# A decoder block's MLP: the down projection by Strassen's seven products in three of four quarters of the width

## Chip, cores and metric

One Trainium2 chip, one core of it. The metric is the device time of one execution in microseconds (us); lower is better. Engines: PE (matrix multiply), ACT (ScalarE), DVE (VectorE), POOL (GpSimd) and SP (which issues most DMA transfers). PE accumulates in PSUM banks of 128 x 512 float32; everything else lies in SBUF.

## The reference, cut to what matters

```python
D_MODEL, SEQ, D_FF = 1024, 512, 4096           # one batch, one layer, all float32
...
x = x + merged @ w_out[i]
h2 = rms_norm(x, norm_mlp_g[i])
x = x + jnp.square(jax.nn.relu(h2 @ w_mlp_up[i])) @ w_mlp_down[i]
return rms_norm(x, norm_final_g)
```

Two mixers (a gated MLP and a state-space scan) come first; the change leaves them alone. It is about the third line: 512 tokens, 1024 -> 4096 -> 1024.

## The kernel before

**Arithmetic.** A float32 product is made of three matmuls. Each operand is split into a rounded part and the rest (`whi`, `wlo` for weights, `ah`, `al` for activations): ACT casts the first (line 118), DVE subtracts (line 119), and `trio` / `mm3` issue lo x hi, hi x lo, hi x hi into one PSUM bank. A weight slab is a tile of 128 x 1024 (512 KB), so each slab costs one cast and one subtraction. `whi` and `wlo` have four buffers each.

**The MLP in quarters.** The hidden width is worked off in four quarters `qd` of 1024 channels. A list `items` says in which order PE takes the work, one slab per item:
- `("c", half)`: the up projection of the first 512 channels, eight plain blocks, in the first quarter only.
- `("p", u, k)`: the up projection of the `u`-th 512 channels is done by Strassen's method: the activation (channels x tokens) and the weights are cut into 2 x 2 blocks, and seven products `k` of block sums take the place of eight. An item is one product: 24 matmuls of 256 columns. The sums of activation blocks (`hq[1..7]`) are made once; the sums of weight blocks are made on the way in, by DMA: `Up.pump` has SP load raw blocks into eight tiles (`ut0` to `ut7`) as these come free, and `Up.sum` has POOL issue transfers that add into a tile (`accum_op`), four for each `u`, two of them from HBM and two from tile to tile. Three products are kept in SBUF (`keep`) and subtracted from a later bank by DVE; `act` then squares the relu on ACT and splits it into `ah`, `al`, which hold a whole quarter.
- `("d", qd, i)`: the down projection, plain: 24 matmuls of 512 columns per slab, eight slabs per quarter; the four finished banks of each half of the output are added to the tokens `x1` by DVE (`res_evac`). Two tiles `wraw` take the raw slabs.

**What sets the order.** The whole MLP stands in a hand-written order. At item `j` the loop first takes the results of item `j-1` out of PSUM, then issues POOL's additions that `sums_at[j]` lists, then splits the slab of item `j+3` (`slabs.take(3)`), then runs what `after[j]` holds (mostly `act`), and last issues the matmuls of `j`. Every engine works its own list strictly in that order. The last slabs go through `tok_major`, whose `fin(1)` also normalises and stores the output, the last token tile in two halves.

```python
items += [("d", qd, 0), ("p", 2 * qd + 1, 4)] + [("d", qd, i) for i in range(1, 8)]
...
for n, d in ((1, 8), (3, 7), (2, 5), (4, 3)) if u % 2 else ((1, 8), (3, 7), (2, 4), (4, 3)):
    sums_at[j - d].append((u, n))
```

Of the kernel before, what the change touches and what calls it, by code (L numbers as in the profile page):

```python
# [11 lines left out]
F32 = mybir.dt.float32  # L12
# [22 lines left out]
H2D = 0, 1.5, 2.5, 5.5, .4, 2.2, .6, 6, 8.5, 8.5  # L35
NR = 4

HALVES, B12 = (0, 2, 1, 3), 6
# [13 lines left out]
def block_kernel(ctx: ExitStack, tc: tile.TileContext, x, w_v, w_all, w_up, wspt, pvec, hvec, g_mix, g_mlp, g_fin, v_g, v_b,  # L52
# [21 lines left out]
    class Slabs:  # L74

        def __init__(self):
            self.ready, self.raws, self.loaded = [], [], 0
            self.todo = collections.deque()
            self.early = False

# [10 lines left out]
        def slab(self):  # L91
            if not self.raws:
                self.load()
            r = parts_of(self.raws.pop(0))
            while self.early and len(self.raws) < 2 and self.loaded < NV + w_all.shape[0]:
                self.load()
            return r
# [732 lines left out]
    class Up:  # L830

        def __init__(self):
            self.free, self.n, self.at = list(tiles), 0, {}

            self.todo = [(0, i) for i in HALVES] + [(1, i) for i in (0, 1, 2, 3, None)]
            self.todo += [(u, i) for u in range(2, 2 * NQ) for i in (2, 3, None, 0, 1)]

        def pump(self):
            while self.free and self.todo:
                t = self.free.pop(0)  # L840
                u, i = self.todo.pop(0)
                nc.sync.dma_start(t, w_up[4 * u + (2 if i is None else i)])
                self.at[u, i] = t

        def sum(self, u, n):

            def add(o, i):
                nc.gpsimd.dma_start(o, i, accum_op=ALU.add)

            self.pump()  # L850
            at = lambda i: self.at[u, i]
            if n == 1:
                add(at(None), w_up[4 * u + 3])
            elif n == 2:
                add(at(0), at(None))
            elif n == 3:
                add(at(2), w_up[4 * u])
            else:
                add(at(1), at(0))

        def make(self, u, k, pair=None):
            self.pump()
            i = {1: 0, 2: 1, 5: None, 6: 0, 3: 1, 7: 2, 4: 3}[k]
            r = parts_of(self.at[u, i], pair)
            if k > 2:
                self.drop(u, i)
            return r
# [11 lines left out]

    up = Up()  # L880
    later = [(0, 1), (0, 2), (0, 5), (0, 6), (0, 3), (0, 7), (1, 1), (0, 4), (1, 2), (1, 5), (1, 6), (1, 3), (1, 7)]


    items = []
    for qd in range(NQ):
        if qd == 0:
            items += [("c", 0)] + [("p", 1, k) for k in (1, 2)] + [("c", 1)] + [("p", 1, k) for k in (5, 6, 3, 7)]
        else:
            items += [("p", 2 * qd + u, k) for u, k in later]
        items += [("d", qd, 0), ("p", 2 * qd + 1, 4)] + [("d", qd, i) for i in range(1, 8)]  # L890
    place = {it: j for j, it in enumerate(items)}

    sums_at = collections.defaultdict(list)
    for u in range(2, 2 * NQ):
        j = place["p", u, 5]
        for n, d in ((1, 8), (3, 7), (2, 5), (4, 3)) if u % 2 else ((1, 8), (3, 7), (2, 4), (4, 3)):
            sums_at[j - d].append((u, n))
    for n, d in ((1, 0), (3, 0), (2, 0), (4, 1)):
        sums_at[d].append((1, n))
    slabs.todo.extend((lambda i=i: up.raw(i)) for i in HALVES)  # L900
    for it in items[4:]:
        slabs.todo.append(slabs.slab if it[0] == "d" else lambda it=it: up.make(*it[1:]))

# [18 lines left out]
    tiles.append(mp.tile([P, SL], F32, name="ut7"))  # L922
    up.free.append(tiles[7])
    gfb = mp.tile([P, DM], F32, name="gfb")
# [17 lines left out]
    def new_act(qd):  # L942
        aTs[qd] = tuple(ap.tile([P, KD, T], F32R, tag=n, name=n, bufs=1) for n in ("ah", "al"))

# [5 lines left out]
    def act(j, u, i, l, src):  # L950

        r_ = mp.tile([P, 2, 256], F32, tag="relu", name="relu", bufs=2)
        nc.scalar.activation(r_, src.rearrange("p (c t) -> p c t", c=2), AF.Relu)
        nc.scalar.activation(r_, r_, AF.Square)
        n = 4 * (u % 2) + 2 * i
# [18 lines left out]
    def act0(j, n, bank):  # L974

        r_ = mp.tile([P, T], F32, tag="relu", name="relu", bufs=2)
        nc.scalar.activation(r_, bank, AF.Relu)
        nc.scalar.activation(r_, r_, AF.Square)
        hi, lo = cut(aTs[0], n)
        nc.scalar.copy(hi, r_)  # L980
        last[j + 1].append(lambda: nc.vector.tensor_sub(lo, r_, hi.bitcast(F32)))

    sums = [[] for _ in range(NT)]

    def fin(nh):
        def evac(t, acc, part=None):
# [12 lines left out]
            if part == 0:  # L999
                return  # L1000
            rs = rms_scale(s)
            o = tiles[1 + t]
            a, b = slice(0, T), slice(T, DM)
            nc.scalar.activation(o[:, a], x1[:, t, a], AF.Copy, scale=rs)
            nc.vector.scalar_tensor_tensor(o[:, b], x1[:, t, b], rs, gfb[:, b], ALU.mult, ALU.mult)
            for c in (a, b):
                nc.sync.dma_start(out[t * P:(t + 1) * P, c], o[:, c])
        return evac
# [3 lines left out]
    for j, it in enumerate(items[:-4]):  # L1012

        if j and items[j - 1][0] == "p":
            _, u, k = items[j - 1]
            evac(j, u, k, BANK.get(k, lambda u: bank_a[u % 2])(u))
        if j == NR:
            wv.flush()
            nr_cm.__exit__(None, None, None)
            ap = ctx.enter_context(pool("act"))  # L1020
# [3 lines left out]
        for u, n in sums_at.pop(j, ()):  # L1024
            up.sum(u, n)
        for f in last.pop(j, ()):
# [3 lines left out]
        else:  # L1030
            w = slabs.take(3)
        for f in after.pop(j, ()):
            f()
# [18 lines left out]
        if it[0] == "p":  # L1052
            _, u, k = it
            if k == 1 and u % 2 == 0 and u:
                new_act(u // 2)
            bank = BANK.get(k, lambda u: bank_a[u % 2])(u)
            for c in range(2):
                for kt in range(4):
                    trio(bank[:, 256 * c:256 * c + 256], wk(w, 4 * c + kt), cut(hq[k], kt),
                         k in (1, 2, 5) and c == 0 and kt == 0, kt == 3)  # L1060
        else:
            _, qd, i = it
# [87 lines left out]
```

## Time and profile before

| | |
|---|---|
| median of 3 runs | 1063.15 us (1062.95 to 1064.41) |
| the profiled execution | 1063.19 us, of which its span (first to last instruction) is 1061.5 us |
| PE busy | 1048.0 us, 99% of the span |
| DVE, ACT, POOL busy | 640.8, 503.8, 163.5 us |
| DMA | 129.76 MB, mean 122 GB/s |

The durations further down are of the profiled execution, which stands 0.04 us from the median. The MLP begins near 725 us. A matmul's printed duration is longer than its distance from the next one, since matmuls overlap; distances are what count on PE.

### The profile page before, as it was taken

The numbers are of one execution on the slowest core, as the hardware profiler recorded it, in microseconds if no ns is written. First come the engines' busy times: TensorE is split into PE (matmuls) and PEld (weight loads), VectorE is DVE, ScalarE is ACT, GpSimd is POOL, SyncE is SP. The second block draws the span as 40 slices with busy tenths as digits, with TensorE's granted clock in tenths as the row PEclk, the third lists the DMA queues.
The fourth block names the chain that finished last, engine by engine and source line by source line (L and its number), as shares of the span: only waits on it lengthen the run. The fifth ranks groups of instructions, "written<-read, shape, count | busy, mean of one in ns | idle before, by whom it ended". The sixth has DMA issues, their size and how long they took to land.

```text
span 1061.5 us, 14620 instructions
## 1 busy us (share of the span) xinstructions
PE 1048.0 (99%) x5709; PEld 908.4 (86%) x5709; DVE 640.8 (60%) x1054; ACT 503.8 (47%) x750; POOL 163.5 (15%) x216
## 2 busy tenths in 40 slices
PE   8999999999999999999999999999999999999997
PEld 7988888888888888888888788879989989988986
DVE  5672455346897996647868975356635634634643
ACT  5743333234547556444465533245824724723742
POOL 3020000001432342300323410002001001101000
PEclk9999999999999999999999999999999999999999
DMA  6433225332333333233233233826737837835232
GB/s 210 141 119 119 80 80 139 99 100 80 100 99 108 106 91 111 82 120 99 80 109 97 71 122 94 299 63 175 206 116 178 219 100 169 232 116 119 62 99 80
DMA packets 39672, 129.76 MB, mean 122 GB/s; under 512 B 4529, under 2 KB 5297, under 8 KB 39602
## 3 DMA queue, kind: packets, MB, share of 16 engines
q1 hardware_dynamic: 35568, 114.13, 34.2%
q0 software_dynamic: 4032, 14.68, 7.5%
q8 instruction: 45, 0.74, 0.3%
q14 instruction: 25, 0.20, 0.1%
q10 hardware_dynamic: 2, 0.00, 0.0%
HBM read 119.30 MB, written 2.16 MB: 114 GB/s over the span
## 4 chain that ended last, share of the span: by engine, by line
PE 79%; DVE 11%; POOL 4%; issue 3%; ACT 2%; DMA 1%; POOLq 0%; SPq 0%; ACTq 0%; DVEq 0%
PE acc L147 15%; PE acc L149 15%; PE acc L148 15%; PE acc L155 14%; PE sm L149 5%; PE sm L147 5%; PE sm L148 5%; DVE cv L570 3%; DVE wlo L119 1%; DVE lm L610 1%; POOL xD L668 1%; PE sm L664 1%; POOL lm L613 1%; POOL yrs L677 1%; PE sm L155 1%
## 5 line engine op out<-in xcount | busy, mean ns | idle before, releaser
L119 DVE TENSOR_TENSOR wlo<-wraw,whi 128x1024 fp32r<-128x1024 f32 (+1 forms) x146 | 175.6, 1204 | 120.8 <-ACT whi L118 120.7
L118 ACT CAST whi<-wraw 128x1024 fp32r<-128x1024 f32 (+1 forms) x146 | 149.8, 1028 | 161.1 <-PE acc L149 73.4
L147 PE MATMUL acc<-hTl,whi 128*128 128x512 f32 x448 | 179.7, 401 | 0.0
L149 PE MATMUL acc<-hTh,whi 128*128 128x512 f32 x448 | 174.8, 390 | 0.0
L148 PE MATMUL acc<-hTh,wlo 128*128 128x512 f32 x448 | 174.6, 390 | 0.0
L119 DVE TENSOR_TENSOR wlo<-ut,whi 128x1024 fp32r<-128x1024 f32 x51 | 62.3, 1224 | 74.5 <-ACT whi L118 74.5
L149 PEld LDWEIGHTS acc<-hTh,whi 128*128 128x128 f32 x448 | 84.1, 188 | 18.0
L148 PEld LDWEIGHTS acc<-hTh,wlo 128*128 128x128 f32 x448 | 84.4, 188 | 15.0
L147 PEld LDWEIGHTS acc<-hTl,whi 128*128 128x128 f32 x448 | 84.4, 188 | 14.8
L147 PE MATMUL sm<-wlo,ah 128*128 128x512 f32 (+1 forms) x232 | 89.5, 386 | 0.0
L149 PE MATMUL sm<-whi,ah 128*128 128x512 f32 (+1 forms) x232 | 89.4, 386 | 0.0
L148 PE MATMUL sm<-whi,al 128*128 128x512 f32 (+1 forms) x232 | 89.4, 385 | 0.0
L118 ACT CAST whi<-ut 128x1024 fp32r<-128x1024 f32 x51 | 53.5, 1051 | 75.2 <-PE sm L149 52.6
L570 DVE SCALAR_TENSOR_TENSOR cv<-acc,pv,cv 128x511 f32<-128x511 f32 (+2 forms) x96 | 71.5, 745 | 29.3 <-ACT cv L568 28.5
L147 PE MATMUL acc<-wlo,hTh 128*128 128x512 f32 (+1 forms) x208 | 77.9, 375 | 0.2
L148 PE MATMUL acc<-whi,hTl 128*128 128x512 f32 (+1 forms) x208 | 75.6, 363 | 0.0
L149 PE MATMUL acc<-whi,hTh 128*128 128x512 f32 (+1 forms) x208 | 75.4, 364 | 0.0
L635 POOL TENSOR_TENSOR xdt<-xb,dt 128x256 f32<-128x256 f32 x32 | 21.9, 685 | 202.0 <-ACT xb L629 197.4
L149 PEld LDWEIGHTS sm<-whi,ah 128*128 128x128 f32 x232 | 43.6, 188 | 8.8
L148 PEld LDWEIGHTS sm<-whi,al 128*128 128x128 f32 x232 | 43.6, 188 | 8.5
L147 PEld LDWEIGHTS sm<-wlo,ah 128*128 128x128 f32 x232 | 43.6, 188 | 8.4
L147 PE MATMUL acc<-yBl,whi 128*128 128x512 f32 x128 | 50.6, 395 | 0.0
(310 smaller groups left out, 2330.7 us busy)
## 6 DMA issues: line engine op xcount, KB each, us to landing
wraw<-in_w_all SPq DMA_DIRECT2D x136, 512.0 KB, 3.6
ut<-in_w_up SPq DMA_DIRECT2D x39, 512.0 KB, 6.7
lm<-csd SPq DMA_DIRECT2D x32, 256.0 KB, 4.5
ut<-in_w_up POOLq DMA_DIRECT2D x14, 512.0 KB, 9.9
ut<-ut POOLq DMA_DIRECT2D x14, 512.0 KB, 4.7
wraw<-in_w_v SPq DMA_DIRECT2D x10, 352.0 KB, 3.2
x<-in_x SPq DMA_DIRECT2D x4, 512.0 KB, 7.2
out<-ut SPq DMA_DIRECT2D x8, 256.0 KB, 2.2
```

The source lines that it names most:

```text
L118: nc.scalar.copy(hi, raw)
L119: nc.vector.tensor_sub(lo, raw, hi.bitcast(F32))
L147: nc.tensor.matmul(o, st[0], mv[1], start=first, stop=False)
L148: nc.tensor.matmul(o, st[1], mv[0], start=False, stop=False)
L149: nc.tensor.matmul(o, st[0], mv[0], start=False, stop=last)
L155: nc.tensor.matmul(o, st[a], mv[b], start=first and i == 0, stop=last and i == 2, skip_group_check=True)
L570: nc.vector.scalar_tensor_tensor(cv[:, s_:], acc[:, :T - s_], cw[:, 3 - s_:4 - s_], cv[:, s_:], ALU.mult, ALU.add)
L610: nc.vector.tensor_scalar(lm[:, j, r, :], lm[:, j, r, :], ncs[:, 2 * hf + j, h0 + r:h0 + r + 1], None, ALU.add)
L613: nc.gpsimd.affine_select(lm, lm, pattern=[[0, 2], [0, R], [1, P]], base=0, channel_multiplier=-1, compare_op=ALU.is_ge, fill=-1e30)
L635: nc.gpsimd.tensor_tensor(xdt, xb4, bc(dt, c), ALU.mult)
L664: nc.tensor.matmul(yp[:, r * HD:(r + 1) * HD], lm[:, r, :], xdt[:, r, :], start=True, stop=True)
L668: nc.gpsimd.tensor_tensor(xD, xD, yv, ALU.add)
```

## The change

In quarters 0, 1 and 2 the down projection is done by seven products as well; quarter 3 keeps the eight plain slabs. An item `("s", qd, k, c)` is one half of the reduction of product `k`: 12 matmuls of 512 columns on one slab, so a product is two items. Its weights are block sums of `w_mlp_down`, made like those of the up projection: raw blocks loaded by SP, four adding transfers by POOL for each half `c`, eight for a quarter. Its activations are block sums too: a quarter's activation now stays whole in float32 (`a`); `down_sum` adds blocks of it in place on DVE, and `down_pair` splits a block into `prh` (ACT) and `prl` (DVE), three buffers of each. A product's two banks are added to or subtracted from `x1` at once by `down_evac`, and bank `a` runs on through products 1, 6, 7 and 4. For two of the `u` (3 and 5) the sums of weight blocks move from POOL's transfers to DVE (`ON_DVE`). The two `wraw` tiles join the eight `ut` tiles. Loads are ordered by when they are needed (`need`). At the very end one small DVE instruction per token tile is folded into another, and the last tile is stored in four pieces.

```diff
+ON_DVE, FINAL = (3, 5), (6, 7)
...
-            items += [("c", 0)] + [("p", 1, k) for k in (1, 2)] + [("c", 1)] + [("p", 1, k) for k in (5, 6, 3, 7)]
+            items += [("c", 0)] + [("p", 1, k) for k in (1, 2)] + [("c", 1)] + [("p", 1, k) for k in (5, 6, 7, 3, 4)]
...
-        items += [("d", qd, 0), ("p", 2 * qd + 1, 4)] + [("d", qd, i) for i in range(1, 8)]
+        if qd == NQ - 1:
+            items += [("d", qd, 0), ("p", 2 * qd + 1, 4)] + [("d", qd, i) for i in range(1, 8)]
+        else:
+            items += [("s", qd, 1, c) for c in range(2)] + [("p", 2 * qd + 1, 4)] * (qd > 0)
+            items += [("s", qd, k, c) for k in (5, 6, 2, 7, 3, 4) for c in range(2)]
...
+            ds = {1: at(5) - 8, 2: at(6) - 6, 3: at(7) - 8, 4: at(3) - 6}
+            for n in ds:
+                sums_at[ds[n]].append(((qd, c), n, False))
...
+            o, a, b, src = {1: (None, 2, 3, 3), 2: (0, 0, None, None), 3: (2, 2, 0, 0), 4: (1, 1, 0, None)}[n]
+            if dve:
+                nc.vector.tensor_add(at(o), at(a), at(b))
             else:
-                add(at(1), at(0))
+                nc.gpsimd.dma_start(at(o), at(b) if src is None else source(u, src), accum_op=ALU.add)
...
+    def down_pair(qd, k):
+        a = aTs[qd]
+        q11, q12, q21, q22 = (a[:, 4 * j:4 * j + 4, 256 * l:256 * l + 256] for j in range(2) for l in range(2))
+        q = {1: q11, 5: q11, 6: q11, 2: q21, 7: q12, 3: q22, 4: q21}[k]
+        hi, lo = prs[k] = tuple(ap.tile([P, 4, 256], F32R, tag=n, name=n, bufs=3) for n in ("prh", "prl"))
+        if k == 1:
+            nc.scalar.activation(hi, q, AF.Copy, scale=-1.0)
+            nc.vector.scalar_tensor_tensor(lo, q, -1.0, hi.bitcast(F32), ALU.mult, ALU.subtract)
+        else:
+            nc.scalar.copy(hi, q)
+            nc.vector.tensor_sub(lo, q, hi.bitcast(F32))
...
+    def down_sum(qd, k):
...
+        if k == 5:
+            nc.vector.tensor_sub(q11, q11, q12)
...
+    def down_evac(k):
+
+        for i, l, bank, op in {1: ((0, 0, "a", "sub"),), 5: ((1, 1, "d", "sub"),), 6: ((0, 1, "a", "sub"),), 2: ((0, 0, "c", "add"),),
+                               7: ((1, 1, "a", "add"),), 3: ((0, 1, "d", "add"),), 4: ((1, 0, "a", "add"),)}[k]:
+            for t in range(2):
+                xs = x1[:, 2 * l + t, i * T:(i + 1) * T]
+                (nc.vector.tensor_sub if op == "sub" else nc.vector.tensor_add)(xs, xs, dbank[bank][t])
...
+        j0 = place["p", 1, 4] if qd == 0 else 0
+        for k, lead, lsum in ((1, 3, None), (5, 3, 4), (6, 3, 3), (2, 3, None), (7, 3, 5), (3, 3, None), (4, 3, 4)):
+            at = place["s", qd, k, 0]
+            if lsum is not None:
+                pairs_at[max(j0, at - lsum)].append((down_sum, qd, k))
+            pairs_at[max(j0, at - lead)].append((down_pair, qd, k))
...
         nc.scalar.activation(r_, bank, AF.Relu)
-        nc.scalar.activation(r_, r_, AF.Square)
-        hi, lo = cut(aTs[0], n)
-        nc.scalar.copy(hi, r_)
-        last[j + 1].append(lambda: nc.vector.tensor_sub(lo, r_, hi.bitcast(F32)))
+        nc.scalar.activation(aTs[0][:, n], r_, AF.Square)
...
-            if sums[t]:
-                nc.vector.tensor_add(s, s, sums[t][-1])
+            nc.vector.tensor_scalar(s, s, 1.0 / DM, sums[t][-1] if sums[t] else EPS, ALU.mult, ALU.add)
...
+        elif j and items[j - 1][0] == "s" and items[j - 1][3] == 1:
+            down_evac(items[j - 1][2])
...
+        for f, *a in pairs_at.pop(j, ()):
+            f(*a)
         for f in after.pop(j, ()):
...
+            bank = dbank[{2: "c", 5: "d", 3: "d"}.get(k, "a")]
+            for t in range(2):
+                for b in range(2):
+                    trio(bank[t], cut(prs[k], 2 * c + b, tsl(t)), wk(w, b, T), k in (1, 2, 5) and c == b == 0, c == b == 1, 1.0)
```

**Two places in the order.** First ACT, in the first quarter, where the last results of the up projection become the first operands of the down projection. Before, `relu`, its square and the cast to `ah` follow each other, and the next slab's cast (`whi`) comes after them:

```order
L980 CAST ah_6656<-relu_6781 128x512
L953 ACTIVATE relu_6785<-kept_6733 128x512
L954 ACTIVATE relu_6785<-relu_6785 128x512
L957 CAST ah_6656<-relu_6785 128x2x256
L118 CAST whi_6817<-wraw_6703 128x1024
L953 ACTIVATE relu_6823<-kept_6696 128x512
L954 ACTIVATE relu_6823<-relu_6823 128x512
L957 CAST ah_6656<-relu_6823 128x2x256
L118 CAST whi_6856<-wraw_6775 128x1024
```

The same stretch of ACT's list with the change. Rows with `whi` are slabs of items to come, `prh_6809`, `prh_6814` and `prh_6876` the rounded operands of products 1, 5 and 6:

```order
L1034 ACTIVATE relu_6775<-kept_6696 128x512
L1037 ACTIVATE a_6657<-relu_6775 128x2x256
L120 CAST whi_6804<-ut2_6117 128x1024
L990 ACTIVATE prh_6809<-a_6657 128x1024
L993 CAST prh_6814<-a_6657 128x1024
L1034 ACTIVATE relu_6818<-kept_6730 128x512
L1037 ACTIVATE a_6657<-relu_6818 128x2x256
L120 CAST whi_6846<-ut3_6118 128x1024
L1034 ACTIVATE relu_6851<-acc_6345 128x512
L1037 ACTIVATE a_6657<-relu_6851 128x2x256
L120 CAST whi_6871<-ut7_6337 128x1024
L993 CAST prh_6876<-a_6657 128x1024
```

The cast per result is gone, and the operand of product 1 stands behind a slab's cast that it did not stand behind before. In the first quarter it is made at the item just ahead of the one that uses it (`j0`), elsewhere three items ahead.

Second DVE, at the same place. Before, between slabs (`wlo`) it makes the rest of each result (`al`), and it touches the tokens four at a time, after eight slabs:

```order
L119 TENSOR_TENSOR wlo_6857<-wraw_6775,whi_6856 128x1024
L119 TENSOR_TENSOR wlo_6887<-wraw_6821,whi_6886 128x1024
L958 TENSOR_TENSOR al_6657<-relu_6892,ah_6656 128x2x256
L119 TENSOR_TENSOR wlo_6923<-wraw_6860,whi_6922 128x1024
L119 TENSOR_TENSOR wlo_6954<-wraw_6890,whi_6953 128x1024
L746 TENSOR_TENSOR x1_5949<-sm_6827,x1_5949 128x512
```

With the change (`wlo_6805` belongs to the third item after the one that runs):

```order
L121 TENSOR_TENSOR wlo_6805<-ut2_6117,whi_6804 128x1024
L991 SCALAR_TENSOR_TENSOR prl_6810<-a_6657,prh_6809 128x1024
L1000 TENSOR_TENSOR a_6657<-a_6657 128x4x256
L994 TENSOR_TENSOR prl_6815<-a_6657,prh_6814 128x1024
L121 TENSOR_TENSOR wlo_6847<-ut3_6118,whi_6846 128x1024
L121 TENSOR_TENSOR wlo_6872<-ut7_6337,whi_6871 128x1024
L1002 TENSOR_TENSOR a_6657<-a_6657 128x4x256
L994 TENSOR_TENSOR prl_6877<-a_6657,prh_6876 128x1024
L1014 TENSOR_TENSOR x1_5949<-x1_5949,sm_6854 128x512
L1014 TENSOR_TENSOR x1_5949<-x1_5949,sm_6855 128x512
```

The sums of activation blocks (L1000, L1002) and the rests `prl` stand between the slabs, and product 1's two banks are taken out (L1014) only after product 6's operand is made.

## Rows read from the trace of the kernel before

**Rows 1.** The page: the span, and PE's busy time.

```profile
span 1061.5 us, 14620 instructions
PE 1048.0 (99%) x5709; PEld 908.4 (86%) x5709; DVE 640.8 (60%) x1054; ACT 503.8 (47%) x750; POOL 163.5 (15%) x216
```

**Rows 2.** The chain that ended last: start us, duration us, what, how many.

```profile
747.27 11.21 PE acc L155 x96
...
804.85 36.75 PE acc L155 x312
847.08 2.83 PE acc L155 x24
887.99 36.75 PE acc L155 x312
```

**Rows 3.** Waits of ACT and DVE, 724 to 1061 us: total us, times, longest.

```profile
ACT whi L118 <- PE sm L149: 99.1, 26, 4.4
...
DVE wlo L119 <- ACT whi L118: 118.9, 68, 4.2
```

**Rows 4.** Timeline of ACT in the first quarter: start us, duration us.

```profile
747.31 1.05 ACT L118 CAST whi<-ut 128x1024 fp32r<-128x1024 f32 x1 [1.75 <-PE sm L155]
748.26 0.63 ACT L953 ACTIVATE relu<-kept 128x512 f32<-128x512 f32 x1
748.92 0.63 ACT L954 ACTIVATE relu<-relu 128x512 f32<-128x512 f32 x1
749.58 0.62 ACT L957 CAST ah<-relu 128x512 fp32r<-128x512 f32 x1
750.13 0.59 ACT L947 COPY kept<-acc 128x512 f32<-128x512 f32 x1
750.62 1.05 ACT L118 CAST whi<-wraw 128x1024 fp32r<-128x1024 f32 x1
```

**Rows 5.** Timeline of DVE, two places: start us, duration us.

```profile
734.66 1.22 DVE L780 TENSOR_TENSOR h<-h 128x1024 f32<-128x1024 f32 x1
735.86 1.23 DVE L767 TENSOR_TENSOR hq7l<-h,hq7h 128x1024 fp32r<-128x1024 f32 x1
...
800.54 1.23 DVE L119 TENSOR_TENSOR wlo<-ut,whi 128x1024 fp32r<-128x1024 f32 x1 [4.22 <-ACT whi L118]
801.68 1.28 DVE L746 TENSOR_TENSOR x<-sm,x 128x512 f32<-128x512 f32 x2
```

**Rows 6.** Stretches of 5 us; the last columns are granted clock, DMA share, GB/s.

```profile
727.00:732.00 5.00, 5.00 (x45) 5.00 (x44) 3.89 (x4) 1.48 (x2) 0.00 (x0) 1.00 1.04 263
...
752.00:757.00 5.00, 5.00 (x45) 5.00 (x44) 3.68 (x5) 4.87 (x9) 0.00 (x0) 1.00 0.91 349
...
800.00:805.00 5.00, 5.00 (x25) 4.18 (x24) 3.23 (x5) 0.61 (x2) 0.00 (x0) 1.00 1.02 177
```

**Rows 7.** DMA issues, 820 to 840 us: count, size, median us to landing.

```profile
ut<-in_w_up SPq DMA_DIRECT2D x5, 512.0 KB, 7.3
ut<-in_w_up POOLq DMA_DIRECT2D x2, 512.0 KB, 10.2
ut<-ut POOLq DMA_DIRECT2D x1, 512.0 KB, 5.1
```

**Rows 8.** The end of the program: timeline, then stretches of 2 us.

```profile
1055.72 0.16 DVE L994 TENSOR_TENSOR fss<-fss 128x1 f32<-128x1 f32 x1 [0.57 <-ACT ut L992]
1055.91 0.15 DVE L228 TENSOR_SCALAR rms_ms<-fss 128x1 f32<-128x1 f32 x1
1056.21 0.55 POOL L230 TENSOR_TENSOR rms_rs<-rms_ms,mhalf 128x1 f32<-128x1 f32 x1 [3.32 <-DVE rms_ms L228]
...
1054.00:1056.00 2.00, 0.58 (x5) 0.38 (x4) 0.76 (x5) 1.02 (x4) 0.00 (x0) 1.00 0.68 262
1056.00:1058.00 2.00, 0.00 (x0) 0.00 (x0) 0.81 (x2) 0.72 (x1) 0.55 (x1) 0.77 0.00 0
1058.00:1060.00 2.00, 0.00 (x0) 0.00 (x0) 0.00 (x0) 0.00 (x0) 0.00 (x0) 0.50 0.68 262
```

More of the change, by code (lines that the diff above doesn't have):

```diff
@@ L94, in slab @@
             r = parts_of(self.raws.pop(0))
-            while self.early and len(self.raws) < 2 and self.loaded < NV + w_all.shape[0]:
+            while self.early and len(self.raws) < 2 and self.loaded < self.end:
                 self.load()
@@ new lines, in block_kernel @@
+    place = {it: j for j, it in enumerate(items)}
+    sums_at, need = collections.defaultdict(list), []
+    for u in range(2, 2 * NQ):
+        j = place["p", u, 5]
+        dve = u in ON_DVE
+        ds = dict(zip((1, 3, 2, 4), ((7, 6, 4, 2) if dve else (8, 7, 5, 3)) if u % 2 else (8, 7, 4, 3)))
+        for n in (1, 3, 2, 4):
+            sums_at[j - ds[n]].append((u, n, dve))
+        s1, m = j - ds[1], lambda k: place["p", u, k] - 3
+        need += [(s1, 0, (u, None), None if dve else 2), (s1 if dve else j - ds[3], 1, (u, 2), 2),
+                 (min(m(1), j - ds[3]), 2, (u, 0), 0), (min(m(2), j - ds[4]), 3, (u, 1), 1), (s1 if dve else m(4), 4, (u, 3), 3)]
@@ L832, in __init__, with source @@
+    need.sort(key=lambda n: n[:2])
+    def source(u, i):
+        return w_up[4 * u + i] if isinstance(u, int) else w_all[DB + 8 * u[0] + 2 * i + u[1]]
+    class Quarters:
         def __init__(self):
-            self.free, self.n, self.at = list(tiles), 0, {}
-            self.todo = [(0, i) for i in HALVES] + [(1, i) for i in (0, 1, 2, 3, None)]
-            self.todo += [(u, i) for u in range(2, 2 * NQ) for i in (2, 3, None, 0, 1)]
+            self.free, self.at = list(tiles), {}
+            self.todo = [((0, i), i) for i in HALVES] + [((1, i), i) for i in range(4)] + [((1, None), 2)]
+            self.todo += [n[2:] for n in need]
@@ L838, in pump @@
         def pump(self):
             while self.free and self.todo:
[L840 to L848, printed above, removed]
+                key, i = self.todo[0]
+                n = next((n for n, t in enumerate(self.free) if not (t in extra and key[0] in FINAL)), None)
@@ L864, in make @@
             r = parts_of(self.at[u, i], pair)
-            if k > 2:
+            if k > 2 and (k != 6 or isinstance(u, int)):
                 self.drop(u, i)
@@ L878, in drop @@
             self.pump()
[L880 to L886, printed above, removed]
-            items += [("c", 0)] + [("p", 1, k) for k in (1, 2)] + [("c", 1)] + [("p", 1, k) for k in (5, 6, 3, 7)]
-        else:
-            items += [("p", 2 * qd + u, k) for u, k in later]
-        items += [("d", qd, 0), ("p", 2 * qd + 1, 4)] + [("d", qd, i) for i in range(1, 8)]
[L891 to L899, printed above, removed]
+    up = Quarters()
     slabs.todo.extend((lambda i=i: up.raw(i)) for i in HALVES)
     for it in items[4:]:
-        slabs.todo.append(slabs.slab if it[0] == "d" else lambda it=it: up.make(*it[1:]))
+        if it[0] == "d":
+            slabs.todo.append(slabs.slab)
+        elif it[0] == "p":
+            slabs.todo.append(lambda it=it: up.make(*it[1:]))
+        else:
+            slabs.todo.append(lambda it=it: up.make((it[1], it[3]), it[2]))
     slabs.early = True
@@ L922, in block_kernel @@
     tiles.append(mp.tile([P, SL], F32, name="ut7"))
-    up.free.append(tiles[7])
+    extra += [wpool.tile([P, SL], F32, tag="wraw", name="wraw", bufs=2) for _ in range(2)]
+    up.free += [tiles[7]] + extra
     gfb = mp.tile([P, DM], F32, name="gfb")
@@ L1000, in evac @@
                 return
-            rs = rms_scale(s)
+            rs = small.tile([P, 1], F32, tag="rms_rs", name="rms_rs", bufs=4)
+            nc.gpsimd.tensor_tensor(rs, s, mhalf, ALU.pow)
             o = tiles[1 + t]
[L1003 to L1007, printed above, removed]
+            w = T // 2 if t == NT - 1 else T
+            for c0 in range(0, T, w):
+                a, b = slice(c0, c0 + w), slice(T + c0, T + c0 + w)
+                nc.scalar.activation(o[:, a], x1[:, t, a], AF.Copy, scale=rs)
+                nc.vector.scalar_tensor_tensor(o[:, b], x1[:, t, b], rs, gfb[:, b], ALU.mult, ALU.mult)
+                for c in (a, b):
+                    nc.sync.dma_start(out[t * P:(t + 1) * P, c], o[:, c])
         return evac
@@ L1054, in block_kernel @@
             if k == 1 and u % 2 == 0 and u:
+                if u // 2 == NQ - 1:
+                    act_cm.__exit__(None, None, None)
+                    ap = ctx.enter_context(pool("act2"))
+                    slabs.loaded, slabs.end = slabs.loaded + 8 * (NQ - 1), NV + w_all.shape[0]
+                    assert not any(t in extra for t in up.at.values())
+                    slabs.load()
+                    slabs.load()
                 new_act(u // 2)
```

69 lines of the change are left out of this document (56 added, 13 removed).

## The prediction

> **What bounds the kernel now.** I read the page's busy times first: PE is busy for 1048.0 of 1061.5 us [rows 1]. Then the chain of waits over the MLP: from 747 us on it is PE alone, one run of matmuls after another. 13 items of 24 narrow matmuls take 36.75 us, so a narrow one follows the next by 117.8 ns and an item takes 2.83 us; behind the single item at 847.08 (to 849.91) the seven down slabs, 168 wide matmuls, last until 887.99: 38.08 us, 226.7 ns each [rows 2]. The view of waits says why the others don't count: ACT's casts waited for PE 26 times (99.1 us), DVE's subtractions for ACT (118.9 us) [rows 3]. Both stand ready and are let go by PE. So in this stage a matmul less is time less, until one of the other engines or the DMA comes last instead. That has to be followed engine by engine.
>
> **The matmuls removed.** Per quarter the plain down projection is 8 slabs x 24 = 192 wide matmuls, the new one 14 items x 12 = 168 of the same width and number of passes. 24 x 226.7 ns = 5.44 us; three quarters: **-16.3 us**. Nothing else leaves PE: the order shows 72 matmuls fewer and no other kind. An "s" item now takes 12 x 226.7 ns = 2.72 us, half of a "d" item, so every lead counted in items is worth half the time it was.
>
> **ACT and DVE in quarters 1 and 2.** Prices: a cast of 1024 columns moves ACT on by 0.95 us (747.31 to 748.26), a relu with its square by 1.32 us (748.26 to 749.58), a `kept` copy by 0.49 us [rows 4]. DVE moves on by 1.14 us after a 1024-column subtraction (800.54 to 801.68) and takes 1.28 us for two banks of tokens, about 0.61 us each back to back; block sums of this strided form cost 1.20 us (734.66 to 735.86), which I round into 1.14 [rows 5]. From product 1 to product 4 there are 14 "s" items and one "p" item, 38.1 + 2.8 = 40.9 us of PE. In them DVE's list has 15 `wlo`, 6 `prl`, 3 block sums and 13 banks of 512: 24 x 1.14 + 13 x 0.61 = 35.3 us, 86%. It fits on average; the place that is tightest is the "p" item in front of product 5: two banks of tokens, `wlo`, the sum for product 6, then a wait until ACT has cast that sum, then `prl`: 0.1 + 1.22 + 1.14 + 1.14 + 1.1 + 1.2 = 5.9 us, against 2.83 us for the item. But its operand is wanted three items later, 8.3 us. Walking on from there item by item with the same prices, DVE is late by up to 5 us, and what is late next is not a slab but a bank: product 6's result must be out of bank `a` before product 7 starts; DVE is done 17.4 us after that item's start, PE comes at 19.2. Cost: 0, with under 2 us to spare. The eight sums that move to DVE (u = 3, 5) fall into "p" items, where DVE has 1.14 us plus a bank now and then to do in 2.83 us: 0. ACT gains 6 slabs and 7 operands and loses 8 short casts per quarter, some 9 us of idle time: 0, except below.
>
> **The first quarter.** Here I find a wait. Four "p" items end at 747.27 + 11.21 = 758.48 [rows 2], the fifth, which now comes directly in front of product 1, at 761.3. ACT at that point has a queue. It may cast the slab three items ahead only when PE has given back its buffer; from 755.7 (the third item done, and the second result of the plain half just squared) it does `whi` 0.95, two results of the plain half and one of the "p" items at 1.31 each, a second `whi` 0.95, and only then `prh` of product 1: 755.7 + 0.95 + 3 x 1.31 + 0.95 + 1.0 = 762.5. DVE has then to finish `wlo` (762.8) and `prl` (764.0). PE can issue one matmul before it needs `prl`: it starts at about 763.8 instead of 761.3, **+2.5 us**. A second one follows: the sum for product 5 (to 765.2), its cast (766.2), two results and two slabs on ACT (770.7), `wlo` (772.0), the sum for product 6 (773.1), its cast (774.2), `prl` (775.4), and only then product 1's first bank (776.0), which product 6 writes on into. PE would be there at 763.8 + 4 x 2.72 = 774.7: **+1.3 us**. After that DVE runs 0.4 to 1 us ahead of PE to the end of the quarter. The bounds of this term: 0, if ACT gets to the third item without a queue, and 3 us more, if those margins break.
>
> **The transfers.** From the loads and additions that the order lists per quarter: 19 loads by SP and 12 additions by POOL of 0.524 MB, 16.25 MB in 39.6 + 38.1 = 77.7 us, 209 GB/s, against 18 + 8 in 83.1 us before, 164 GB/s. Within the "s" stretch it is 10 + 9, 9.96 MB in 40.9 us, 243 GB/s. Mixed traffic at a full share moved 263 GB/s, loads almost alone 349, additions alone 177 [rows 6]. So the stretch runs at some nine tenths of what the rows show, with a pause after it (12 of 31 transfers in the other half). An addition from HBM landed after 10.2 us, one from tile to tile after 5.1 us [rows 7]; they are issued five and three items (13.6 and 8.2 us) ahead of the split, which is itself 8.2 us ahead of PE. I take 0. For the other end see the third rival.
>
> **The tail.** One small DVE instruction leaves the last chain: 1055.72 to 1055.91, -0.19 us [rows 8]; the store in halves I take at 0, bounds +-0.3.
>
> **Sum.** The profiled execution is 1063.19 us (span 1061.5 and 1.7 around it), as good as the median of 1063.15. 1063.2 - 16.3 + 2.5 + 1.3 - 0.2 = **1050.5 us**.
>
> **Rivals.** *First: no wait in the first quarter.* The cast of `prh` depends on results that are ready by 758; if ACT's queue is shorter than I count, only matmuls and tail remain: 1063.2 - 16.5 = 1046.7. Against it: the queue is added up from rows.
>
> *Second: the waits of the first quarter in all three.* The same two places exist in quarters 1 and 2, with less than 2 us of margin at the banks. If DVE's back-to-back prices don't hold because each instruction waits for ACT (118.9 us of such waits now [rows 3]), every quarter loses up to 3.8 us: 1058.1; half of that in two quarters, 1054.3. The clock belongs here: where PE had no work at the very end, the granted clock went to 0.77 over 1056 to 1058 and 0.50 after, 1.2 instead of 2.4 GHz [rows 8]. If a hole brought that on, one product at the lower level would cost 5.4 us more. The gap in the first quarter is broken by a matmul, so I don't count it.
>
> *Third, the other side: the additions hold up the weights.* If the "s" stretch moved only what additions alone do, 177 GB/s [rows 6], a quarter's 16.25 MB would need 92 us, 14 us more than PE; in two to three quarters 28 to 42 us, 1079 to 1093. It decides from 16.25 MB / (77.7 + 6.4 us) = 193 GB/s on, where two quarters eat the 12.7 us that are left. For it: eight more additions per quarter, four where DVE took over. Against it: 263 GB/s in the nearest mixture. The Trainium skill, in "DMA: Bandwidth & Descriptors", section "Issuing engines are not separate DMA queues", speaks for it: transfers of SP and POOL run on the same 16 engines and interleave, so a second issuer buys no bandwidth. The trace agrees in so far as an SP load took 7.3 us beside additions [rows 7]. The same page's "Specifications" put the ceiling at 435 GB/s; by it, as an estimate, the stretch would need 23 of its 40.9 us and this rival would be out. The rows stay far below that figure while additions run, so the rival keeps its chance.
>
> **How the numbers follow.** Forecast 0.52, its own range 1048.5 to 1053; first rival 0.15; second 0.18; third 0.09; the rest, 0.06, lies between them on the faster side or near no change. The range 1046.4 to 1057 takes in the first rival, the forecast and most of the second, some 0.83. Faster by over 0.2% (2 us, about what a measurement tells from no change): 0.52 + 0.15 + 0.18 + 0.03 = 0.88; within it 0.03; slower 0.09.
>
> **What would show it.** Right: 168 wide matmuls per quarter still 227 ns apart; in the first quarter two idle stretches of PE, 2.5 us ahead of the first wide matmul, ended by DVE's `prl`, and about 1.3 us ahead of product 6, ended by the subtraction from `x1`; none in quarters 1 and 2; ACT's waits for PE much shorter than 99.1 us. Wrong: PE idle behind ACT's `whi` that itself waited for a transfer (third rival), idle stretches ahead of products 6 and 7 in the later quarters or a granted clock under 1.00 (second), or no idle stretch at all (first).

## The result, and the profile after

| | before | after |
|---|---|---|
| median | 1063.78 us (4 runs, 1062.95 to 1064.41) | 1058.03 us (4 runs, 1056.58 to 1059.09) |
| profiled execution | 1063.19 us, span 1061.5 | 1057.3 us, span 1055.6 |

The ratio is 0.9946 (95% interval 0.9928 to 0.9963): faster by 5.75 us (0.5%), where 12.7 were forecast. The time is 7.5 us over the forecast and 1.0 us over its range.

The page of after, which answers to [rows 1]: 72 matmuls fewer, as forecast, but 21.5 us of the span without PE instead of 13.5.

```profile
span 1055.6 us, 14639 instructions
PE 1034.1 (98%) x5637; PEld 896.4 (85%) x5637; DVE 700.0 (66%) x1108; ACT 527.7 (50%) x766; POOL 178.6 (17%) x232
```

The view of waits of after, 715 to 1056 us, for PE: total us, times, longest. Before, PE had 0.3 us of waits in the same stretch.

```profile
PE acc L157 <- ACT kept L1028: 4.9, 3, 2.4
PE sm L157 <- ACT whi L120: 1.0, 1, 1.0
PE sm L157 <- DVE prl L991: 0.9, 1, 0.9
PE sm L157 <- ACT prh L990: 0.9, 1, 0.9
PE sm L788 <- DVE rms_h L805: 0.8, 1, 0.8
```

The last four rows are the two waits of the first quarter that the prediction had, and the entry. The first row is new, and the largest: PE waits for ACT's `kept` copies, in which the prediction saw no danger. The same view for ACT (720 to 1050 us) answers to [rows 3]:

```profile
ACT whi L120 <- PE sm L157: 19.7, 15, 1.7
ACT whi L120 <- DMA ut<-ut: 19.2, 7, 4.3
...
ACT whi L120 <- DMA wraw<-ut: 6.4, 2, 4.7
...
ACT whi L120 <- DMA ut<-wraw: 3.5, 1, 3.5
```

ACT stood ready for PE 99.1 us before [rows 3], now 19.7; instead it stands 29.1 us behind transfers, and every one of the ten is an addition from tile to tile, none a load of SP. Before there was one such wait, of 2.1 us, for a load.

Where PE idles, from its timeline (the distance to the matmul before, less the regular one, with the 0.1 us by which the next matmul follows late):

| where | forecast | after |
|---|---|---|
| 72 matmuls of 226.7 ns | -16.3 | -16.3 |
| ahead of product 1 of the first down projection (765.45, 766.88) | +2.5 | +2.35 |
| ahead of its product 6 (778.88) | +1.3 | +1.28 |
| ahead of the up projection's product 7, first quarter (755.82) | 0 | +2.59 |
| ahead of product 3 in quarters 1, 2, 3 (820.01, 897.94, 976.07) | 0 | +2.64, +0.22, +0.43 |
| entry of the MLP (724.30) | 0 | +0.68 |
| from the last result in `x1` to the end | -0.2 | +0.27 |
| sum | -12.7 | -5.8 (span: -5.9) |

How such a stretch comes about, in the timeline of POOL, ACT and PE of after, near 820 us (start us, duration us, engine, line, operation, in brackets the idle time before it and what ended it):

```profile
802.65 0.88 POOL L903 DMA_DIRECT2D ut<-ut  x1 [13.46 <-DVE wlo L121]
...
808.98 1.05 ACT L120 CAST whi<-ut 128x1024 fp32r<-128x1024 f32 x1 [4.28 <-DMA ut<-ut]
...
809.41 0.88 POOL L903 DMA_DIRECT2D wraw<-ut  x1 [5.89 <-issue]
...
815.25 1.05 ACT L120 CAST whi<-wraw 128x1024 fp32r<-128x1024 f32 x1 [4.74 <-DMA wraw<-ut]
...
819.39 0.57 ACT L1028 COPY kept<-acc 128x512 f32<-128x512 f32 x1
...
820.01 0.39 PE L157 MATMUL acc<-hq3l,whi 128*128 128x256 f32 x1 [2.38 <-ACT kept L1028]
```

The addition for product 6 writes into the tile that product 1 reads unchanged. So POOL can't issue it before VectorE has split that tile (`wlo`, the releaser in the first row): at 802.65. ACT comes to it at 804.70 (808.98 less 4.28). PE would have let the cast go at 806.2, where product 1 begins (820.01, less 2.53 of idle time and four items of 2.83), but ACT stands until the addition has landed, 6.3 us after its issue. The next addition, for product 3, starts after that and holds ACT from 810.51 to 815.25. ACT takes its list in order, so product 5's copy stands at 819.39, and product 3, which wants that bank, is 2.6 us late. The same places in the kernel before:

```profile
791.18 0.88 POOL L848 DMA_DIRECT2D ut<-ut  x1 [48.84 <-DVE wlo L119]
...
804.89 1.05 ACT L118 CAST whi<-ut 128x1024 fp32r<-128x1024 f32 x1 [4.38 <-PE sm L149]
```

There 13.7 us lay between issue and cast, and ACT was released by PE. The split of product 6 may go three items after that of product 1: three "d" items are 16.3 us (3 x 5.44), three "s" items 8.2, and what ACT and DVE are late with product 1's split comes off that. So the room for this addition has shrunk from 13.7 to 3.5 us (802.65 to 806.2), while the transfer takes 6.2 to landing. The same addition before, issued at 791.18, took 4.4 (the 5.1 of [rows 7] are those of another one).

### The profile page after: what moved, and what is told of

Its sections match the earlier page's. It is cut to its first block, busy times and chain, and to the rows that moved or that the text cites. A ratio compares the mean times of both kernels' runs of the same rounds, so it can differ in the third digit from the quotient of the medians.

```text
span 1055.6 us, 14639 instructions
## 1 busy us (share of the span) xinstructions
PE 1034.1 (98%) x5637; PEld 896.4 (85%) x5637; DVE 700.0 (66%) x1108; ACT 527.7 (50%) x766; POOL 178.6 (17%) x232
## 5 line engine op out<-in xcount | busy, mean ns | idle before, releaser
L121 DVE TENSOR_TENSOR wlo<-wraw,whi 128x1024 fp32r<-128x1024 f32 (+1 forms) x138 | 165.8, 1203 | 94.0 <-ACT whi L120 93.9
L120 ACT CAST whi<-wraw 128x1024 fp32r<-128x1024 f32 (+1 forms) x138 | 141.4, 1026 | 131.1 <-PE acc L151 76.1
L121 DVE TENSOR_TENSOR wlo<-ut,whi 128x1024 fp32r<-128x1024 f32 x77 | 93.6, 1224 | 48.8 <-ACT whi L120 48.6
L120 ACT CAST whi<-ut 128x1024 fp32r<-128x1024 f32 x77 | 80.3, 1049 | 63.2 <-DMA ut<-ut 19.2
L157 PE MATMUL sm<-wlo,prh 128*128 128x512 f32 x144 | 56.3, 391 | 1.9 <-ACT whi L120 1.0
L157 PE MATMUL sm<-whi,prl 128*128 128x512 f32 x144 | 56.1, 390 | 0.9 <-DVE prl L991 0.9
L157 PE MATMUL sm<-whi,prh 128*128 128x512 f32 x144 | 56.1, 389 | 0.0
L151 PE MATMUL acc<-yBh,whi 128*128 128x512 f32 x128 | 49.9, 390 | 0.0
L150 PE MATMUL acc<-yBh,wlo 128*128 128x512 f32 x128 | 49.9, 390 | 0.0
L149 PEld LDWEIGHTS acc<-wlo,hTh 128*128 128x128 f32 x208 | 39.3, 189 | 5.1 <-issue 1.2
```

The lines of the kernel that those rows point to most:

```text
L120: nc.scalar.copy(hi, raw)
L121: nc.vector.tensor_sub(lo, raw, hi.bitcast(F32))
L149: nc.tensor.matmul(o, st[0], mv[1], start=first, stop=False)
L150: nc.tensor.matmul(o, st[1], mv[0], start=False, stop=False)
L151: nc.tensor.matmul(o, st[0], mv[0], start=False, stop=last)
L157: nc.tensor.matmul(o, st[a], mv[b], start=first and i == 0, stop=last and i == 2, skip_group_check=True)
```

## The experiments

The theory: ACT stands behind additions that can't start before product 1's split and have only three items' room, and the copies behind it hold PE up. The rivals: the order of the first quarter's products, VectorE's own lateness, and the mere number of transfers. Single profiles are compared by their idle stretches, since the entry of the MLP alone lies between 724.87 and 726.34 us in the two kernels without this change and between 725.31 and 727.66 in those with it. A stretch is given with the 0.1 us behind it, and PE's granted clock is 1.00 where nothing else is said.

**1. The order of the first quarter.**

```
-... for k in (5, 6, 7, 3, 4)]
+... for k in (5, 6, 3, 7, 4)]
```

> The changed kernel with product 3 back between products 6 and 7 in the first quarter (5, 6, 3, 7, 4). Theory A, the order: product 7 stands directly behind product 6 in one bank, so the copy of product 6 has no item to hide behind; with product 3 between them the 2.5 us of idle PE ahead of product 7 (755.8 us) go, and nothing of over 0.3 us takes their place until product 1 of the down projection: total about 2 us less, 1056. Theory B, ACT is held up on a weight cast that waits for an addition: the copies of products 5 and 6 come late whatever stands next; the idle stretch moves ahead of product 3, which wants the bank of product 5, and is 1 to 1.5 us, total about 1 us less, 1057. In both the idle stretch of 2.5 us near 820 us stays.

Measured 1057.12 us. The stretch ahead of product 7 is gone; 0.40 us stand ahead of product 3, and 1.84 ahead of product 4, released by VectorE's subtraction of product 7 from the same bank (the waits of PE):

```profile
PE acc L157 <- ACT kept L1028: 3.4, 3, 2.6
PE acc L157 <- DVE kept L1053: 1.6, 1, 1.6
```

The delay moved, nearer to B, and the neighbours in one bank are now 7 and 4. Near 820 it is 2.88.

**2. The early loads of the down projection later.** `wraw` tiles and `ut7` go to the loads at the fifth item.

```
-    up.free += [tiles[7]] + extra
...
         if j == NR:
+            up.free += [tiles[7]] + extra
```

> The three tiles that become free at the entry of the MLP are handed to the loads only at the fifth item, so that the three early loads of the down projection don't run beside the first additions. Theory B with contention: the first two additions land within 11 us instead of 13 to 14.6, the two that follow from tile to tile are done before ACT comes to them, ACT waits for no transfer near 750, and the idle PE ahead of product 7 (755.8 us) falls from 2.5 to under 1 us; the idle 2.5 us near 820 may change with the order of the later loads. Rival, the additions are late by themselves (they are issued late, or the read from HBM is slow): the landing times and the 2.5 us stay. Total 1055.5 to 1056.5 by the first, unchanged at 1057.3 by the rival.

Measured 1058.35 us. The first two additions landed after 11.2 us (14.6 in after, 11.0 before), and 0.93 us stand ahead of product 7. That part is as expected, but the tiles are dealt out otherwise later on: 3.1 us near 819 and 1.29 at 977, and something new behind the first of these. The stretches of 2 us, with the granted clock third from the end:

```profile
816.00:818.00 2.00, 0.00 (x0) 0.00 (x0) 2.00 (x4) 1.14 (x2) 0.00 (x0) 1.00 0.97 295
818.00:820.00 2.00, 1.35 (x7) 1.36 (x8) 2.00 (x2) 2.00 (x5) 0.00 (x0) 0.70 0.76 279
820.00:822.00 2.00, 2.00 (x11) 2.00 (x11) 2.00 (x3) 0.97 (x2) 0.88 (x1) 0.50 0.90 254
822.00:824.00 2.00, 2.00 (x18) 2.00 (x18) 1.16 (x3) 0.69 (x1) 0.00 (x0) 0.95 0.94 117
```

After the idle stretch the clock is at its lower level, 1.2 GHz, for some 3 us; 16 narrow matmuls follow each other by 213 ns instead of 118, another 1.5 us.

**3. The even half-quarters' tile to tile sums on VectorE.**

```
-            sums_at[j - ds[n]].append((u, n, dve))
+            sums_at[j - ds[n]].append((u, n, dve or (u % 2 == 0 and n in (2, 4))))
```

> In the even half-quarters (2, 4, 6) the two block sums of tile to tile additions are done by VectorE instead of by transfers. Theory B: ACT's casts stop waiting for additions there (19.2 us of such waits in the changed kernel, some 4 us of them left near 750), the copy of product 5 is on time, and the idle 2.5 us near 820 go to under 0.4; the 2.5 us at 755.8 and the 2.4 and 1.2 us in front of products 1 and 6 of the first down projection stay; total about 2 to 2.5 us less, 1055. Rival, VectorE itself is late there (it comes out of the first quarter's waits behind its list): two more subtractions of 1.14 us for it make the idle stretch near 820 as long or longer, and similar ones appear near 898 and 976; total 1057 to 1061.

Measured 1052.98 us. ACT's waits for additions fall from 29.1 to 4.4 us (its waits, 720 to 1050 us):

```profile
ACT whi L120 <- DMA ut<-ut: 2.6, 1, 2.6
ACT whi L120 <- DMA wraw<-ut: 1.8, 1, 1.8
```

No idle stretch of over 0.1 us is left anywhere behind 778 us. VectorE, with six more block sums that the rival said it had no time for, delays nobody. Ahead of product 7 there stand 0.93 us.

**4. The kernel before with product 7 directly behind 6.**

```
-... for k in (5, 6, 3, 7)]
+... for k in (5, 6, 7, 3)]
```

> The kernel before, with product 7 directly behind product 6 in the first quarter (5, 6, 7, 3), nothing else. It measures the order by itself, without the extra loads and additions. Theory A, the order alone costs what is seen in the changed kernel: PE idle for about 2.5 us ahead of product 7, total 1065.5. Theory B, the order alone costs only the copy's own way (the end of the last matmul to the end of one copy, 0.6 to 0.9 us), and the rest comes from ACT being held up on an addition, which here lands in time: idle 0.6 to 0.9 us, total 1064.

Measured 1066.15 us beside 1064.06, with an entry 1.47 us later than in the profile of before. The timeline of PE shows the one stretch, 1.46 us with its successor:

```profile
755.49 0.39 PE L155 MATMUL acc<-hq7l,whi 128*128 128x256 f32 x1 [1.20 <-ACT kept L947]
```

It lies between the two figures. ACT waits for no addition here; its list ahead of this copy just holds two casts of `ah` (0.62 us each) that the changed kernel hasn't. So the order costs 0.9 us in the new list (runs 2 and 3), and what the changed kernel has beyond that is the addition.

**5. All sums as transfers,** the opposite of the third.

```
-ON_DVE, FINAL = (3, 5), (6, 7)
+ON_DVE, FINAL = (), (6, 7)
```

> The changed kernel with all block sums of the up projection as transfers, those of the half-quarters 3 and 5 too. It is the opposite of the third experiment: if a tile to tile addition costs PE where it has less than its 6 us between the split that frees its tile and the split that reads it, the half-quarters 3 and 5 stand behind narrow items of 2.83 us, as in the kernel before, and get no idle stretch, and those near 820, 898 and 976 us stay: total 1056.5 to 1058.5. If the number of transfers is what matters (contention), eight more per two quarters make the stretches near 898 and 976 grow to 2 us or more and new ones appear: total 1059 to 1064.

Measured 1067.66 us, slower than before (1064.5 beside it) and over both ranges, with 2.05 us of it from a later entry (727.59, 725.54 in after). The stretches ahead of product 3 are 4.9, 1.7 and 2.2 us, a new one of 0.6 stands at 925, and after the first and the last the clock was at 0.50 for a while. Near 820 the additions landed after 7.1 and 6.9 us (6.2 and 5.8 in after). So the number of transfers does count, but by way of the same wait: each addition takes longer in a room that is too short for it.

**6. The first quarter's lists,** on top of the third: product 1's operand directly behind the plain half's results, the one result that stood ahead of it now behind it, the sum for product 6 (`f6`) earlier.

```
+    f6 = (down_sum, 0, 6)
+    pairs_at[place["s", 0, 6, 0] - 3].remove(f6)
+    pairs_at[place["p", 1, 4] + 1].append(f6)
...
+            jj += jj == place["p", 1, 4] - 1
             after[jj]...
...
+            if j == place["p", 1, 4]:
+                down_pair(0, 1)
+                pairs_at[j].remove((down_pair, 0, 1))
             w = slabs.take(3)
```

> The kernel of the third experiment (even block sums on VectorE), and in the first quarter ACT casts product 1's operand right behind the two results of the plain half, ahead of one more result (1.2 us) and of a slab (0.94 us), and the sum for product 6 is made before the slabs that stood ahead of it. If the two waits of the first down projection are ACT's and DVE's lists, as the prediction had them, the 2.35 us ahead of product 1 fall to under 0.5 and the 1.2 us ahead of product 6 to under 0.5: total about 1050. If they hang on something else (the results of the up projection, or DVE with too much to do whatever its order), they shrink by less than half or come back at products 6 or 7: total 1052 to 1053.

Measured 1054.44 us. Ahead of product 1 there are 0.19 us left of 2.35; so that wait was ACT's list, as the prediction added it up. Product 6's stays at 1.36, against what was expected. Ahead of product 7 the addition was late again (2.04 us), and 17 matmuls after it ran at the lower clock; with an entry 0.9 us later, that is why the total is over that of the third.

**7. The order 6, 5, 7, 3, 4,** on top of the third, so that the two banks take turns.

```
-... for k in (5, 6, 7, 3, 4)]
+... for k in (6, 5, 7, 3, 4)]
```

> The kernel of the third experiment with the first quarter's products in the order 6, 5, 7, 3, 4, so that the two PSUM banks take turns and every copy has an item to hide behind. The idle stretch ahead of product 7 (0.83 us in the third experiment, 2.5 in the changed kernel) goes to under 0.2; none appears ahead of products 3 and 4, as it did with 5, 6, 3, 7, 4. The 2.4 and 1.2 us of the first down projection stay within 0.5. Total 1052. If ACT's wait for the last addition reaches PE in this order too, an idle stretch of 1 to 2 us stands ahead of one of these products and the total is 1053 to 1054.

Measured 1052.24 us: no idle stretch ahead of any of these products. The waits ahead of product 1 stay (2.35, and the lower clock behind them: 0.53 over 766 to 768).

**8. Runs 6 and 7 together.**

> The two before together: even block sums on VectorE, the order 6, 5, 7, 3, 4, product 1's operand first, the sum for product 6 earlier. If the idle stretches are independent, PE has under 1 us of idle time between 730 and 1045 us and the total is 1049 to 1050, which is what the matmuls alone give less the entry and the tail; if one gives back another, 1051 to 1053.

Measured 1050.14 us, just over what was expected of independent stretches. Ahead of product 6 there are 1.36 us left, ahead of product 1 0.30.

**9. The changed kernel once more.**

> The changed kernel once more, nothing edited: which of its idle stretches belong to the kernel and which to one execution. The 2.4 and 1.2 us of the first down projection should stand within 0.1 of the first profile. The stretch ahead of product 7 (755.8 us) should vary between 0.8 and 2.5 us, as it did in the experiments that left its instructions alone (2.5, 0.8, 1.7), and that near 820 stay at 2.5 to 3; where a stretch brings the granted clock to its lower level, 1.4 to 2.2 us come on top. If the cost of the first quarter is fixed by the order of the list alone, the stretch ahead of product 7 is 2.5 us again.

Measured 1057.94 us (4 runs, 1056.72 to 1059.14; ratio 0.9941, 0.9926 to 0.9956). Ahead of products 1 and 6 it is 2.35 and 1.28 again, ahead of product 7 now 1.16, near 820 3.1 us. This time the clock fell after it:

```profile
818.00:820.00 2.00, 0.38 (x1) 0.38 (x2) 2.00 (x3) 1.97 (x4) 0.00 (x0) 0.84 0.99 360
820.00:822.00 2.00, 2.00 (x11) 2.00 (x11) 2.00 (x3) 1.95 (x3) 0.16 (x1) 0.50 0.62 188
```

So the waits on lists belong to the kernel, and those on additions vary from execution to execution. Between the two profiled ones (1057.30 and 1059.14 us) the stretches of product 3 make +1.3 us, the clock +1.4, the entry +0.7 and the stretch ahead of product 7 -1.4. The other executions have no profile, so what makes up the whole spread of 2.5 us isn't shown.

**10. The third, timed.**

> The third experiment timed in rounds: even block sums on VectorE. By its one profile PE loses 2.5 us less near 820 and nothing at 898 and 976, and up to 1.7 us less ahead of product 7, which is chance: 2 to 4.5 us under the changed kernel, 1053 to 1056, 0.990 to 0.993 of the kernel before. If the one run was an exception, it is within 1 us of the changed kernel.

Measured 1054.17 us, 0.991 of before (0.9893 to 0.9928): 1052.43 and 1052.62, and 1055.73 and 1055.93. Over the whole span the mean granted clock was 0.999 in the first two and 0.997 and 0.996 in the others. Only a run of the first kind has a profile: 0.94 us ahead of product 7, clock 1.00.

**11. Everything together,** with two results squared while ACT would wait for the sum for product 5, and the end of the program as before.

```
             w = slabs.take(3)
+        if j == place["p", 1, 4]:
+            for f in after.pop(j, ()):
+                f()
```

> Everything that worked together (even block sums on VectorE, the order 6, 5, 7, 3, 4, product 1's operand first), two results of the up projection squared while ACT would wait for the sum for product 5, and the end of the program as in the kernel before. The idle 1.3 us ahead of product 6 should fall under 0.5, and the end of the program be 0.2 to 0.3 us shorter: total 1048 to 1049.5, 0.985 to 0.987 of the kernel before. If the wait ahead of product 6 is PSUM's bank and not the list ahead of it, it stays and the total is 1049.5 to 1050.5.

Measured 1047.69 us (4 runs, 1047.48 to 1047.81), 0.9844 of before (0.983 to 0.9859), a little better than expected. The waits of PE, 715 to 1056 us, have one row left, the entry's (0.30 us ahead of product 1 are too scattered for one):

```profile
PE sm L788 <- DVE rms_h L805: 0.3, 1, 0.3
```

From the MLP's entry to the end it takes 320.35 us (725.65 to 1046.0), 336.63 before (724.87 to 1061.5): 16.28 less, the whole of the matmul term.

**12. The same with the even sums as transfers again.**

```
-            sums_at[j - ds[n]].append((u, n, dve or (u % 2 == 0 and n in (2, 4))))
+            sums_at[j - ds[n]].append((u, n, dve))
```

> The best kernel with one part undone: the even block sums are transfers again, the first quarter stays mended. It asks why the idle stretch near 820 us (2.5 to 2.9) is longer than the two that follow it by quarters (0.2 to 0.6 and 0.3 to 1.2). If VectorE, late out of the first quarter, frees the tile for the addition late, a first quarter without waits brings the first stretch down to that of the others, under 0.6, total 1048.5 to 1049.5. If the room between the split that frees the tile and the split that reads it is too short whatever VectorE does, 2 to 3 us stay near 820 and 0.2 to 1.2 at the other two, total 1050.5 to 1053.

Measured 1052.17 us, with 1.81, 0.20 and 0.43 us ahead of product 3. It answers neither way: 0.8 us of the first stretch went with the first quarter's waits, as VectorE's lateness would have it; 1.8 did not. POOL and ACT at the same places, first and second quarter after the first:

```profile
797.94 0.88 POOL L903 DMA_DIRECT2D ut<-ut  x1 [13.46 <-DVE wlo L121]
...
803.95 1.05 ACT L120 CAST whi<-ut 128x1024 fp32r<-128x1024 f32 x1 [3.19 <-DMA ut<-ut]
...
876.43 0.88 POOL L903 DMA_DIRECT2D ut<-ut  x1 [13.54 <-DVE wlo L121]
...
882.00 1.05 ACT L120 CAST whi<-ut 128x1024 fp32r<-128x1024 f32 x1 [1.73 <-PE sm L157]
```

In the second, 5.6 us lie between issue and cast, and that is just enough: PE is the releaser. In the first 6.0 us lie between them. PE would have let the cast go at 802.2 (815.25, where product 3 begins, less the wait of 1.71 and four items of 2.83), 4.3 us after the issue. The 1.7 us that are missing are the stretch. Why the room is 1.3 us shorter in the first stays open: VectorE is busy without a break ahead of both (21.00 us of 777 to 798 and of 855.5 to 876.5), so this run doesn't rule its lateness out.

## Why the prediction was wrong

*The matmuls* (-16.3): right. Run 11, without waits, is 16.28 us shorter from the entry on.

*The first quarter's two waits* (+2.5, +1.3): right in place and size (+2.35, +1.28, both again in run 9). The first is ended by the instructions that were named, and run 6 removes it by the order of ACT's list. For the second the view of waits names ACT's `whi`, and not the subtraction from `x1` that was forecast:

```profile
778.05 1.28 DVE L1014 TENSOR_TENSOR x<-x,sm 128x512 f32<-128x512 f32 x2
778.88 0.47 PE L157 MATMUL sm<-wlo,prh 128*128 128x512 f32 x1 [1.05 <-ACT whi L120]
```

That cast (777.74 to 778.77) is of a slab three items ahead, which product 6 doesn't read. The first of the two subtractions, which frees the bank, ends at 778.73, 0.15 us before PE starts, and by the program PE must wait for it. So the forecast's reading fits, though the profile's label doesn't say it. Run 6 moved the sum for product 6 and left this wait as it was (1.36); run 11 ends it by having ACT square two results during its wait for the sum for product 5 (2.63 us in run 8, 0.25 in run 11), which lets the rest of the chain that was forecast begin earlier.

*ACT and DVE in quarters 1 and 2* (0): right for DVE. It is full there, 21.00 of 21.0 us busy from 860 to 881 and from 938 to 959, and late as said: in quarter 1 product 6's banks are empty 17.1 us after the start of the "p" item (851.04 to 868.14), where 17.4 were forecast. PE comes for them at 870.2, and no bank that DVE has to empty stops PE in those quarters. For ACT it was wrong: "0, except below" counted its work and not what it stands behind.

*The transfers* (0): **this is the step that failed.** It took the additions as issued "five and three items (13.6 and 8.2 us) ahead of the split", that is by their place in the program. The addition for product 6 writes into a tile that must be split for product 1 first, and the one for product 3 waits for that addition; so near 820 us there were 3.5 us for the first of them, and 6.3 passed from its issue to the cast. The prediction had said in so many words that a lead in items is worth half its time now, and didn't apply it to this one. It looked only for a bank that VectorE empties late; it is ACT's copy that was late. It cost 3.3 us in quarters 1 to 3, with some VectorE lateness in it (0.8 us by run 12), and 2.6 in the first. There the additions run beside the new early loads and land late (14.6 us against 11.2; run 2 shows it), and product 7 stood right behind 6 in one bank. That new order, for which the prediction has no term, is 0.9 of the 2.6 us (runs 2 and 3); the rest varies with the execution.

*The tail* (-0.2): wrong by 0.5. From the start of the last addition to `x1` to the end it was 6.78 us before, 7.05 after. Over all profiles the old end takes 6.61 to 6.97 (before, runs 4, 11 and 12) and the new one 6.92 to 7.30 (after and the nine other runs), so it is longer in the main, and a single execution tells it to some 0.3 us. One small VectorE instruction is gone, but the halves take longer than the whole: two outputs of 128x256 0.91 us on ACT, where one of 128x512 took 0.72, and SP issues four stores. No run undoes one of the two by itself.

```profile
1049.90 0.55 POOL L1083 TENSOR_TENSOR rms_rs<-fss,mhalf 128x1 f32<-128x1 f32 x1 [3.23 <-DVE fss L1075]
1050.48 0.91 ACT L1088 ACTIVATE ut<-x,rms_rs 128x256 f32<-128x256 f32 x2 [0.97 <-POOL rms_rs L1083]
...
1051.00 2.18 SPq L1091 DMA_DIRECT2D out<-ut  x4
```

*The entry* (+0.68) had no step. It seems to belong to the execution: run 9, the same kernel, enters another 0.74 us later (726.28), though its wait for `rms_h` is 0.3 us and that of after 0.8.

*The rivals.* The third had the mechanism, ACT's cast behind a transfer, but its price by bandwidth was far off (28 to 42 us): ACT waited for no load, and the "s" stretch moved about what it was said to need (246 GB/s over 781.5 to 807 us, 234 over 860 to 881, where 243 were counted). What was short was time between two dependent steps. By the Trainium skill, "DMA: Bandwidth & Descriptors", section "Issuing engines are not separate DMA queues", transfers issued by different engines share the same 16 DMA engines; the trace agrees in so far as the addition for product 6 landed later beside more traffic. The stretches from its issue to its landing, before and after (the last columns are granted clock, DMA share, GB/s):

```profile
791.18:795.60 4.42, 4.42 (x21) 3.67 (x20) 0.50 (x1) 1.05 (x1) 0.88 (x1) 1.00 0.60 119
802.65:808.85 6.20, 6.20 (x40) 5.58 (x39) 4.46 (x6) 1.05 (x1) 0.88 (x1) 1.00 0.77 224
```

With the 4.4 us of before it would have landed at 807.05, still 0.9 us after PE was ready (806.2). So of the 2.8 us by which the cast came late, 1.8 go with the longer landing and 0.9 with the room alone; by themselves 1.8 us more would have been hidden in a room of 13.7. The second rival's waits came in the first quarter only. Its remark on the clock came true in other executions, and in run 7 for the very gap that the prediction left out because a matmul breaks it.

## What to carry to other kernels

When items become shorter, every dependence whose lead is counted in items has to be priced again in time, transfers first; the lead of a transfer starts at the last reader of the tile that it writes, not at its place in the program. A copy out of a PSUM bank that stands in an in-order list behind a wait is as late as that wait, so look for what stands behind each instruction that can wait for DMA. And give two products that follow each other different banks.

## What was not expected of the hardware

Whether an idle stretch brings PE's clock to 1.2 GHz wasn't told by its length (given here without the 0.1 us behind it). After 2.53 us (after, 820), 2.48 (after, product 7) and 2.77 (run 1) it stayed at 1.00, and the next matmuls kept their 118 ns; after 2.84 (run 9), 2.98 (run 2), 2.06 and 4.63 (run 5) and even 1.94 (run 6) it fell to 0.50 for about 3 us, about 5 after the longest, which cost 1.4 to 2.2 us each time. The 2.35 us ahead of product 1, broken by one matmul, were followed by the lower clock in run 7 (1.6 us), and not in after or in runs 2, 3, 5, 9 and 10. The row of after that answers to those of runs 2 and 9:

```profile
820.00:822.00 2.00, 1.99 (x16) 1.99 (x17) 2.00 (x3) 2.00 (x3) 0.00 (x0) 1.00 0.84 246
```

What decides it stays open. So a wait of 2 to 3 us may cost half as much again or more, and differently in each execution; run 11, without them, spreads over 0.3 us, where the changed kernel spreads over 2.5.
